# Four edits to the order of one encoder layer's work: a residual load, a fold, a norm and a chain of sums

## The chip, the cores and the metric

The kernel runs on one core of a Trainium2 chip. The time is device microseconds (us) of one execution; for the kernel before it is the median of three runs. The engines are named as the profile names them: PE is TensorE's matmuls, PEld its weight loads, DVE is VectorE, ACT is ScalarE, POOL is GpSimd, and SP is SyncE, which only issues transfers here.

## The reference

One layer of a bidirectional encoder is applied to two groups of tokens with the same weights: "prompt" (1024 tokens) and "sample" (512 tokens), each with 16 meta tokens ahead, which are dropped at the end. Model width 1024, hidden width 4096, fp32.

```python
h = rmsnorm(x, g_mix)
q, k, v, u, gate_na, gate_fn = split(h @ w_in)
y_na = neighbourhood_attention(q, k, v, rel_bias, meta_bias) @ w_branch_na
y_fn = fourier_mix(u) @ w_branch_fn      # real part of a 2-D DFT, positions x channels
mixed = sigmoid(gate_na) * y_na + sigmoid(gate_fn) * y_fn
x = x + mixed @ w_out
a = relu(rmsnorm(x, g_mlp) @ w_up)
y = rmsnorm(x + (a * a) @ w_down, g_final)
```

## The kernel before, in words

Every fp32 product is made of three products of rounded halves (`mm3`, its matmuls at L132): a value x is split into hi = round(x) and lo = x - hi. A weight block of 512 KB is loaded (`weights`, L149, a transfer on SP), cast to hi by ACT (L155), and lo is subtracted by POOL, or by DVE where that is asked for (L157). PE runs almost without a break. There are eight PSUM banks of 512 columns: pairs named ps_mm, ps_s, ps_o and ps_t. Three names (mm, s, o) are handed out in turn to products, and ps_t takes transposes and, in places, products.

`Layer.run` takes the sample first and then the prompt. The stages of the sample are: reading rows with their norm and transposes, attention, `gates` (13 products with columns of w_in, counted from P0), `merge_na` (8 blocks of W_na), the Fourier branch (`fourier_channels`, `fourier_positions`), `merge_fn` (blocks of W_fn and the transposed gate), `project_out` (w_out, the residual, a norm, transposes) and `Up` (32 products f0 to f31 with columns of w_up). The prompt follows with the same stages, and at the end the class `Halves` does the prompt's up projection and the down projection of both groups by a Strassen-like scheme.

The program is written in one order, and a scheduler puts the instructions of each engine into a queue, so what is written late may be queued earlier. Two helpers bind it: `behind(marks)` keeps what is inside it behind the marked instructions, and `pinned()` keeps it behind the last instruction written so far on every engine. Each queue is then worked off strictly in order.

The places that matter here:

- `fold_u` (L248) makes two matrices: a step of loads (the DFT matrix and four blocks of `w_uT`), then eight folds, each of four 128x128 matmuls (L259), three ACT and three DVE evictions and two stores to `wu`. `gates` calls such side steps after its products: a triple (steps, first, end) in `beside` means one step after each product from number `first` up to `end`. `folded` (L869) later loads `wu` back on POOL's queue.
- `merge_na` loads W_na block by block into a tile named relu (L825). `fn_ahead` loads the blocks of `w_fnA` and `w_fnB` (L866), adds and subtracts them and stores the result `wfn` (L860).
- `project_out` adds into four residual tiles `acc` (128x1024, 512 KB each), loaded from the sample's rows at L1091. In the trace these loads stand among W_na's.
- `Up.run` calls `next(reading)` after each pair of products from f2 and f3 on. `reading` is the generator `read` (L277) on the prompt's rows: load a row tile (L288, with a gain load after the first), transpose the tile before (`transpose_in`, L194 on PE, copies at L136 and L137), and `norm` (a square with its sum on ACT at L178, a root at L179, five DVE operations L180 to L184). It has one buffer for the row and one for the normed row. Between these, `combine` loads rows of w_down, subtracts and adds on POOL and stores the sums t2 (L1194).
- `down` (in `Halves`) goes through steps (n, u). A step makes six products, one to a bank. At the last u of an n, each bank is evicted by a DVE add (L1639), and then `load(i + 2)` makes the operands of the step after next: up to four DVE sums of W_down's blocks (L1613, 128x1024), the ACT casts and the POOL or DVE lo parts.

The functions that the change touches, and what calls them:

Of the kernel before, what the change touches and what calls it, by code (L numbers as in the profile page):

```python
# [17 lines left out]
F32 = mybir.dt.float32  # L18
# [8 lines left out]
D = 1024  # L27
# [41 lines left out]
class Layer:  # L69
# [280 lines left out]
    def run(self, order):  # L350
        nc = self.nc
# [3 lines left out]
        hp, close_hT = self.open("hT_0", "left")  # L355
        hT, folded = self.new_hT(hp, order[0][1], NM)
        for i, (name, T) in enumerate(order):
            nxt = order[i + 1] if i + 1 < len(order) else None
            small = T <= 512
# [3 lines left out]
            if i == 0:  # L363
                with pool("first", "right") as p:
                    gain = p.tile([128, D], F32, name="gain")
                    reading = self.read(name, T, hT, lambda: p.tile([128, D], F32, name="xt", bufs=3),
                                        lambda: p.tile([128, D], F32, name="hn", bufs=2), gain)
# [5 lines left out]
                    marks = self.mark((mybir.EngineType.SP,))  # L373
                    w0 = self.qk_weights(0)

                    rest = self.tables(marks)
# [20 lines left out]
            if small:  # L397
                ap, hp_, mp = (right.enter_context(pool(f"{n}_{name}", "right")) for n in ("acc", "hid", "mlp"))
                fn = right_fn.enter_context(pool(f"fn_{name}", "right"))
# [7 lines left out]
            else:  # L407
                fn = None
# [10 lines left out]
            if small:  # L419
                wide = lambda: [fn.tile([128, n], F32R, name=f"wu{n}")[:, :1040].rearrange("p (a b) -> p a b", a=4) for n in (1040, 1072)]  # L420
                flat = lambda pair: [t.rearrange("p a b -> p (a b)") for t in pair]
                beside = [(self.fold_u(mp.tile([128, 512], F32, name="relu", bufs=2)[:, :128],
                                       [t.bitcast(F32) for _ in range(2) for t in flat(self.pair(mp, [128, 2, 512]))],
                                       lambda: flat(self.pair(fn, [128, 4, 128], bufs=4))), 0, 9),
                          (fold, 5, 13)]
            near_end = self.gates(T, hT, mixed, sig, lambda pr: self.weights(
                od[pr], oT[pr], raw=hp_.tile([128, T], F32R, name="hid_hi", bufs=4) if small else "raw"), beside)
            sin = []
# [25 lines left out]
            with self.pinned():  # L454
                for _ in ahead:
                    pass
            if not small:
                close_sin()
            out = ExitStack()
# [13 lines left out]
            if not small:  # L473
# [4 lines left out]
                right_fn.close()  # L478
                Halves(self, name, T).run(right, hp_, mp, h2T, self.wo + rest)
                continue  # L480
            acc = [ap.tile([128, D], F32, name=f"acc{t}") for t in range(T // 128)]
            self.short = mlp = self.Up(self, ap, hp_, mp, name, T, h2T)
            marks = self.mark()
            with self.behind(marks):
                rest = list(wout)
            self.project_out(hp_, mp, self.ins[f"x_{name}"], T, h2T, rest, acc, mlp, marks)
            out.close()
            right_fn.close()
            reading, before_last = iter(()), lambda qs: None
# [591 lines left out]

            yield self.weights(src, place and (place() if callable(place) else self.pair(*place)), lo_engine=self.nc.vector if i == 2 else None)

    def project_out(self, hp, p, x, T, m, wo, acc, mlp, marks):

        nc = self.nc
        wo = self.wo + wo
        nt = T // 128
        gain = self.gain(p.tile([128, D], F32, name="gain", bufs=1), "g_mlp")
        for t in range(nt):  # L1090
            nc.sync.dma_start(acc[t], x[t * 128:(t + 1) * 128, :])  # L1091
        pending = []

        def product(ps, half, t, blocks, more=False):
            ts = slice(t * 128, (t + 1) * 128)
            w = wo[4 * half:4 * half + 4]
            self.mm3(ps, [(m[kt // 2][0][:, kt % 2, ts], m[kt // 2][1][:, kt % 2, ts], w[kt // 2][0][:, kt % 2], w[kt // 2][1][:, kt % 2])
                          for kt in blocks], more=more)
            return ps


        banks = {(0, t): product(self.psum(), 0, t, range(6)) for t in range(2)}
        for half in range(2):
            cs = slice(half * 512, (half + 1) * 512)
            for t in range(nt):
                if (half, t) in banks:
                    ps = product(banks[half, t], half, t, range(6, 8), True)
                else:
                    ps = product(self.psum(), half, t, range(8))
                nc.vector.tensor_tensor(out=acc[t][:, cs], in0=acc[t][:, cs], in1=ps, op=ALU.add)  # L1110
                if half:
                    nc.sync.dma_start(mlp.sums[t], acc[t])
                    if len(pending) == 2:
                        self.transpose_in(*pending.pop(0))
                    hn = hp.tile([128, D], F32, name="hn", bufs=2)
                    self.norm(acc[t], gain, hn, junk=p.tile([128, 512], F32, name="relu", bufs=2).bitcast(BF16))
                    pending.append((hn, m, t * 128))
                    if t == nt - 2:
                        with self.behind(marks):
                            mlp.load(0)  # L1120
        mlp.load(1)
        mlp.load(2)
        for f in range(3):
            next(mlp.ups[f])
            if pending:
                self.transpose_in(*pending.pop(0))

    class Up:
# [68 lines left out]
        def run(self, reading, before_last):  # L1197
            layer = self.layer
            combining = self.combine()
            for g in range(self.NF // 2):  # L1200
                if g == self.NF // 2 - 5:
                    marks = layer.mark()
                if g == self.NF // 2 - 2:
                    for _ in reading:
                        pass
                    for f in range(2 * g, 2 * g + 2):
                        self.load(f)
                    with layer.behind(marks):
                        before_last((0, 1))
                for f in range(2 * g, 2 * g + 2):  # L1210
                    for _ in self.ups[f]:
                        pass
                    if f == self.NF - 2:
                        self.load(f + 1)
                        with layer.pinned():
                            before_last((2, 3))
                with layer.pinned():
                    next(combining, None)
                if g:
                    next(reading, None)  # L1220


class Halves:
# [357 lines left out]
    def down(self, p):  # L1581
# [23 lines left out]
                                    lambda: p.tile([128, 2, TH], F32R, name="long", bufs=2)] + [stream] * 4)  # L1605

        def load(i):
            if i >= len(steps):
                return
            rs, rl, rw, *rest = (x.bitcast(F32) for x in self.raws.pop(i))  # L1610
            n, u = steps[i]
            for x, (_, sign) in zip(rest, self.parts(self.DOWN[n][1], u)[1:]):
                nc.vector.tensor_tensor(out=rw, in0=rw, in1=x, op=ALU.add if sign > 0 else ALU.subtract)  # L1613
            if i < 2:
                x, *others = self.take(5)
                ws = [x[:, k * 2 * SH:(k + 1) * 2 * SH].rearrange("p (a b) -> p a b", a=2) for k in range(2)]
                wl, ww = ([x.rearrange("p (a b) -> p a b", a=2) for x in others[k:k + 2]] for k in (0, 2))
            else:
                ws, wl, ww = (layer.pair(p, [128, 2, w], k, 3) for k, w in (("hs", SH), ("h", TH), ("w", 512)))
            todo = [(rs, ws, nc.vector), (rl, wl, nc.vector), (rw, ww, nc.vector if i == 0 else None)]  # L1620
            done = [layer.split_sb(x, *to, lo_engine=lo) for x, to, lo in (todo if rest else todo[::-1])]
            got[steps[i]] = tuple(done if rest else done[::-1])
# [96 lines left out]
        for i, (n, u) in enumerate(steps):  # L1719
            if u == 0 and n not in self.ON_TOP:  # L1720

                banks = []
                for _ in range(nh):
                    banks.append(layer.psum(("mm", "mm", "s", "s", "t", "t", "o", "o")[used % 8]))
                    used += 1

            with layer.behind(self.stored if i < 6 else []):
                fetch(i + 2)

            if u < nu - 1:  # L1730
                with layer.pinned():
                    load(i + 2)
            if n in (1, 2) and u < nh:
                with layer.pinned():
                    acc[n - 1][u] = self.tile(places[(n - 1) * nh + u])
                    nc.sync.dma_start(acc[n - 1][u], tiles[n - 1][u][0])
            if (n, u) == (3, 0):
                gain = layer.gain(self.tile("gain"), "g_final")
            if n == len(self.DOWN) - 1 and u >= nu - apart:
                continue  # L1740
            for t in range(nh):
                product(banks[t], t, n, [u])
                if u == nu - 1:
                    evict(n, t)
            with layer.pinned():
                if u == nu - 1:
                    load(i + 2)
                elif late:
                    late.pop(0)()
                elif n == 5 and u < nh:  # L1750
                    begin_last(u)
# [90 lines left out]
```

## Time and profile before

| | |
|---|---|
| median of 3 runs | 1930.3 us (1929.49 to 1931.05) |
| the profiled execution's own time | 1930.41 us |
| its span (first to last instruction) | 1928.6 us |
| granted TensorE clock, mean | 0.998 |
| PE busy | 1892.7 us (98%) |
| DVE, ACT, POOL busy | 1117.6, 751.5, 823.2 us |
| moved by DMA | 358.38 MB, 186 GB/s over the span |

1.8 us of the profiled time lie outside the span. In a row of the timeline the first two numbers are the start and the length in us, then come engine, line, operation, output<-inputs, shape and count; in square brackets stands how long the engine had been idle just before and what ended that. "SPq" is SP's queue issuing a transfer. Matmuls overlap in the pipeline, so the start of one row and the end of the row before can cross.

### The profile page before, as it was taken

To read this page: it belongs to the slowest core of one execution; us is meant where nothing else is said; L and a number is where in the kernel's file an instruction comes from. 1 tells how busy PE (TensorE), PEld (TensorE's weight loads), DVE (VectorE), ACT (ScalarE), POOL (GpSimd) and SP (SyncE) were. 2 spreads that over 40 slices of the span, in tenths; PEclk is the share of its full clock that TensorE was granted. 3 is DMA by queue.
4 is the path that set the end of the run, shared out by engine and by line. 5 is a ranking of instruction groups with operands and counts; after the bars stand their busy time and mean duration, and the time that the engine had idled before them with its cause. 6 is when DMAs were issued, how large, how long until landed. Compare 5 with 4: busy or idle time off the path is not lost.

```text
span 1928.6 us, 26107 instructions
## 1 busy us (share of the span) xinstructions
PE 1892.7 (98%) x9435; PEld 1588.4 (82%) x9435; DVE 1117.6 (58%) x1747; ACT 751.5 (39%) x1351; POOL 823.2 (43%) x676
## 2 busy tenths in 40 slices
PE   7999999999999999999999999999999999999998
PEld 5888888888888888888898878888888888888886
DVE  5771554787626566660527375656565326758856
ACT  3674333444215565542223243333333333333334
POOL 1334553555512232342224217988882323323531
PEclk9999999999999999999999999999999999999999
DMA  6757873687765455463452422444446778568733
GB/s 221 195 148 236 228 232 121 213 272 254 237 195 162 125 137 153 136 229 87 129 154 88 164 99 96 179 174 156 174 163 244 274 249 289 199 219 285 273 118 127
DMA packets 312945, 358.38 MB, mean 186 GB/s; under 512 B 51768, under 2 KB 222392, under 8 KB 312264
## 3 DMA queue, kind: packets, MB, share of 16 engines
q1 hardware_dynamic: 295056, 334.93, 52.6%
q0 software_dynamic: 17760, 21.80, 5.0%
q8 instruction: 74, 1.21, 0.3%
q14 instruction: 55, 0.45, 0.1%
HBM read 263.06 MB, written 96.16 MB: 186 GB/s over the span
## 4 chain that ended last, share of the span: by engine, by line
PE 88%; DVE 4%; DMA 3%; ACT 2%; issue 1%; POOL 1%; SPq 0%; DVEq 0%; ACTq 0%; POOLq 0%
PE ps_mm L132 23%; PE ps_o L132 22%; PE ps_s L132 19%; PE ps_t L132 11%; PE ps_mm L531 3%; PE ps_mm L532 3%; PE ps_mm L533 3%; PE ps_o L680 2%; DMA relu<-in_w_na 1%; PE ps_t L660 1%; PE ps_t L194 1%; PE ps_s L647 0%; PE ps_s L648 0%; DMA vf_sample<-vd_sample 0%; DMA gate_prompt<-ot 0%
## 5 line engine op out<-in xcount | busy, mean ns | idle before, releaser
L157 POOL TENSOR_TENSOR w_lo<-w_raw,w_hi 128x1024 fp32r<-128x1024 f32 x69 | 177.1, 2566 | 218.6 <-ACT w_hi L155 160.2
L157 POOL TENSOR_TENSOR w_lo<-raw,w_hi 128x1024 fp32r<-128x1024 f32 (+1 forms) x49 | 100.6, 2056 | 203.3 <-ACT w_hi L155 197.4
L155 ACT CAST w_hi<-w_raw 128x1024 fp32r<-128x1024 f32 x88 | 92.4, 1050 | 175.9 <-PE ps_s L132 48.0
L157 DVE TENSOR_TENSOR h_lo<-long,h_hi 128x1024 fp32r<-128x1024 f32 x54 | 77.2, 1429 | 93.6 <-ACT h_hi L155 93.6
L531 PE MATMUL ps_mm<-hT,w_hi 128*128 128x512 f32 (+2 forms) x296 | 121.5, 410 | 0.0
L532 PE MATMUL ps_mm<-hT,w_hi 128*128 128x512 f32 (+2 forms) x296 | 110.4, 373 | 0.0
L533 PE MATMUL ps_mm<-hT,w_lo 128*128 128x512 f32 (+2 forms) x296 | 110.3, 373 | 0.0
L155 ACT CAST h_hi<-long 128x1024 fp32r<-128x1024 f32 x54 | 56.7, 1050 | 103.2 <-PE ps_s L132 26.7
L157 DVE TENSOR_TENSOR hs_lo<-short,hs_hi 128x512 fp32r<-128x512 f32 x54 | 73.2, 1355 | 13.4 <-ACT hs_hi L155 12.3
L155 ACT CAST w_hi<-raw 128x1024 fp32r<-128x1024 f32 (+1 forms) x49 | 40.9, 840 | 101.6 <-DVE raw L1613 54.4
L654 ACT ACTIVATE sc<-sc,ast 128x288 f32<-128x288 f32 (+4 forms) x96 | 53.9, 561 | 68.3 <-DVE ast L652 68.0
L1397 POOL TENSOR_TENSOR x<-w_hi,x 128x512 fp32r<-128x512 f32 (+1 forms) x42 | 70.9, 1688 | 16.4 <-ACT x L1400 16.4
L680 PEld LDWEIGHTS ps_o<-pt,vb 104*64 104x64 f32 (+6 forms) x576 | 62.4, 163 | 10.1 <-POOL vb L617 2.7
L680 PE MATMUL ps_o<-pt,vb 104*64 104x128 f32 (+6 forms) x576 | 62.3, 243 | 2.1 <-POOL vb L617 1.4
L533 PEld LDWEIGHTS ps_mm<-hT,w_lo 128*128 128x128 f32 x296 | 55.7, 188 | 10.4
L132 PE MATMUL ps_t<-gate,x 128*128 128x512 f32 x264 | 63.7, 390 | 0.0
L617 POOL TENSOR_TENSOR vb<-vr,vb 96x384 fp32r<-96x384 f32 (+4 forms) x48 | 48.5, 1029 | 34.7 <-ACT vb L616 31.1
L132 PE MATMUL ps_mm<-gate,x 128*128 128x512 f32 x256 | 62.6, 389 | 0.0
L774 POOL MEMSET bm<- 64x96 f32 (+2 forms) x64 | 11.1, 174 | 117.7 <-DVE ast L652 103.2
L652 DVE CUSTOM_DVE_ANT_0 sc<-ps_s,bm 128x288 f32<-128x288 f32 (+4 forms) x96 | 46.3, 482 | 23.1 <-issue 10.6
L132 PEld LDWEIGHTS ps_t<-gate,x 128*128 128x128 f32 x264 | 49.4, 188 | 10.9 <-DVE r_lo L1510 0.7
L532 PEld LDWEIGHTS ps_mm<-hT,w_hi 128*128 128x128 f32 x296 | 56.2, 190 | 1.6
(706 smaller groups left out, 5578.6 us busy)
## 6 DMA issues: line engine op xcount, KB each, us to landing
long<-hidden_prompt SPq DMA_DIRECT2D x54, 512.0 KB
w_raw<-in_w_in SPq DMA_DIRECT2D x52, 512.0 KB
raw<-in_w_down SPq DMA_DIRECT2D x39, 512.0 KB
w_raw<-in_w_up SPq DMA_DIRECT2D x34, 512.0 KB
hidden_prompt<-h SPq DMA_DIRECT2D x32, 512.0 KB
short<-hidden_sample SPq DMA_DIRECT2D x54, 256.0 KB
w_lo<-in_w_down SPq DMA_DIRECT2D x18, 512.0 KB
w_raw<-in_w_out SPq DMA_DIRECT2D x16, 512.0 KB
```

Of the source, the lines that this page charges most:

```text
L132: self.nc.tensor.matmul(out, a, b, start=(i == 0 and not more), stop=(i == len(terms) - 1), skip_group_check=more)
L155: nc.scalar.copy(out=hi, in_=raw)
L157: (lo_engine or nc.gpsimd).tensor_tensor(out=lo, in0=raw, in1=hi.bitcast(F32), op=ALU.subtract)
L194: nc.tensor.transpose(tp[:, i * 128:i * 128 + n], hn[:n, kt * 128:(kt + 1) * 128], self.ident[:n, :n])
L531: nc.tensor.matmul(ps, a[0], b[0], start=(kt == 0), stop=False)
L532: nc.tensor.matmul(ps, a[0], b[1], start=False, stop=False)
L533: nc.tensor.matmul(ps, a[1], b[0], start=False, stop=(kt == 7))
L617: nc.gpsimd.tensor_tensor(out=lo, in0=vs, in1=hi.bitcast(F32), op=ALU.subtract)
L652: nc.vector.tensor_tensor_reduce(out=sc[:, :W], in0=ps[:, :W], in1=bm[:, :W], scale=1.0, scalar=3e38, op0=ALU.add, op1=ALU.min, accum_out= ...
L654: nc.scalar.activation(out=sc[:, :W], in_=sc[:, :W], func=AF.Exp, bias=st[:, 0:1], scale=-1.0, accum_out=st[:, 1:2])
L680: nc.tensor.matmul(po[:m, j * 128:(j + 1) * 128], v, x, start=(i == 0), stop=(i == len(ops) - 1))
L1397: self.nc.gpsimd.tensor_tensor(out=to, in0=x, in1=y, op=op)
```

## The change

Four edits, in four places:

1. `fold_u`'s loads stay behind product P0 of the sample's gates; its eight folds stand behind P2 to P9 instead of P1 to P8.
2. The sample's four residual row tiles are loaded in `run`, right after the last step of `fn_ahead` and pinned there, instead of in `project_out`, from where the scheduler had drawn them forward.
3. In `Up.run` the call of `next(reading)` after f3 (g = 1) is bound behind the last instructions written so far on SP, ACT, POOL and DVE. That call loads the prompt's first row tile and norms it.
4. In `down`, the sums of `load(i + 2)` at the last u of an n are made one after each eviction, pinned there, instead of all after the sixth eviction. The casts and lo parts stay behind the last sum.

```diff
-                beside = [(self.fold_u(mp.tile([128, 512], F32, name="relu", bufs=2)[:, :128],
+                beside = [self.fold_u(mp.tile([128, 512], F32, name="relu", bufs=2)[:, :128],
                                        [t.bitcast(F32) for _ in range(2) for t in flat(self.pair(mp, [128, 2, 512]))],
-                                       lambda: flat(self.pair(fn, [128, 4, 128], bufs=4))), 0, 9),
-                          (fold, 5, 13)]
+                                       lambda: flat(self.pair(fn, [128, 4, 128], bufs=4)))]
+                beside = [(*beside, 0, 1), (*beside, 2, 10), (fold, 5, 13)]
...
             with self.pinned():
                 for _ in ahead:
                     pass
+                if small:
+                    acc = [ap.tile([128, D], F32, name=f"acc{t}") for t in range(T // 128)]
+                    for t in range(T // 128):
+                        nc.sync.dma_start(acc[t], self.ins[f"x_{name}"][t * 128:(t + 1) * 128, :])
...
-            acc = [ap.tile([128, D], F32, name=f"acc{t}") for t in range(T // 128)]
             self.short = mlp = self.Up(self, ap, hp_, mp, name, T, h2T)
...
-            self.project_out(hp_, mp, self.ins[f"x_{name}"], T, h2T, rest, acc, mlp, marks)
+            self.project_out(hp_, mp, T, h2T, rest, acc, mlp, marks)
...
-    def project_out(self, hp, p, x, T, m, wo, acc, mlp, marks):
+    def project_out(self, hp, p, T, m, wo, acc, mlp, marks):
...
-        for t in range(nt):
-            nc.sync.dma_start(acc[t], x[t * 128:(t + 1) * 128, :])
...
                 if g:
-                    next(reading, None)
+                    with layer.behind(layer.mark() if g == 1 else []):
+                        next(reading, None)
...
         def load(i):
+            for _ in load_parts(i):
+                pass
+
+        def load_parts(i):
...
                 nc.vector.tensor_tensor(out=rw, in0=rw, in1=x, op=ALU.add if sign > 0 else ALU.subtract)
+                yield
...
+            loading, sums = iter(()), 0
+            if u == nu - 1 and i + 2 < len(steps):
+                loading = load_parts(i + 2)
+                sums = len(self.parts(self.DOWN[n + 1][1], 1)) - 1
             for t in range(nh):
                 product(banks[t], t, n, [u])
                 if u == nu - 1:
                     evict(n, t)
+                    if t < sums:
+                        with layer.pinned():
+                            next(loading, None)
             with layer.pinned():
                 if u == nu - 1:
-                    load(i + 2)
+                    for _ in loading:
+                        pass
```

Three places show what this does to the queues; the line numbers are of the kernel whose order it is.

**PE in the sample's `Up`, around f5 and f6.** gate holds the normed hidden input, r the prompt's normed row tile 0. Before:

```order
L132 MATMUL ps_mm<-gate,w_hi 128x512 x16
L132 MATMUL ps_mm<-gate,w_lo 128x512 x8
L194 MATMUL ps_t<-ident,r_3972 128x128 x8
L132 MATMUL ps_s<-gate,w_hi 128x512 x16
L132 MATMUL ps_s<-gate,w_lo 128x512 x8
```

and in the changed kernel:

```order
L132 MATMUL ps_mm<-gate,w_lo 128x512 x8
L132 MATMUL ps_s<-gate,w_hi 128x512 x16
L132 MATMUL ps_s<-gate,w_lo 128x512 x3
L194 MATMUL ps_t<-ident,r_3972 128x128 x8
L132 MATMUL ps_s<-gate,w_lo 128x512 x5
L132 MATMUL ps_o<-gate,w_hi 128x512 x16
```

The eight transposes of the prompt's first row tile stood ahead of f6 and now stand after 19 of its 24 matmuls. Those of the second and third tile stand inside f8 and f10 in the same way (after 19 and 7 matmuls); from the fourth tile on they stand between products, as before.

**SP in the sample's `Up`.** Before, the first row's load (L288) stood among the sums' stores at the end of `project_out`:

```order
L1112 DMA sum_sample_3360<-acc_3348 128x1024
L1112 DMA sum_sample_3361<-acc_3349 128x1024
L288 DMA r_3969<-in_x_prompt 128x1024
L170 DMA r_3830<-in_g_mix 128x1024
L1112 DMA sum_sample_3362<-acc_3350 128x1024
L149 DMA w_raw<-in_w_up 128x8x128 x2
L288 DMA r_4061<-in_x_prompt 128x1024
L1168 DMA hidden_sample_3351<-hid_hi 128x2x256
```

and in the changed kernel:

```order
L1169 DMA hidden_sample_3355<-hid_lo 128x2x256
L1177 DMA hidden_sample_3355<-hn 128x4x256
L1195 DMA t_0_3893<-acc_3895 128x512
L288 DMA r_3969<-in_x_prompt 128x1024
L170 DMA r_3830<-in_g_mix 128x1024
L1169 DMA hidden_sample_3356<-hid_hi 128x2x256
L149 DMA w_raw<-in_w_up 128x8x128 x2
```

The first row's load now stands behind the stores of the second pair (f2, f3) and behind the first store of t2.

**SP at the end of the Fourier branch.** acc is a residual tile, gain at the first row a buffer that holds half of W_fn's rows. In the changed kernel:

```order
L869 DMA gain<-in_w_fnB 128x4x128
L460 DMA acc_3151<-in_x_sample 128x1024
L460 DMA acc_3152<-in_x_sample 128x1024
L863 DMA wfn_3145<-raw 128x512
L863 DMA wfn_3149<-raw 128x512
L460 DMA acc_3153<-in_x_sample 128x1024
L460 DMA acc_3154<-in_x_sample 128x1024
L149 DMA w_raw<-in_w_out 128x2x512 x2
L170 DMA gain<-in_g_mlp 128x1024
L149 DMA w_raw<-in_w_out 128x2x512 x6
```

The four residual loads stood two and two between W_na's last blocks (issued at 229.58 and 233.32 us in the trace before; the W_fn row that opens this piece was issued at 269.87), and one w_out load stood directly behind that W_fn row. Now all four stand ahead of every w_out load.

## The prediction

> **What bounds the kernel now.** I read the page first, its busy times and its chain.
>
> ```profile
> span 1928.6 us, 26107 instructions
> PE 1892.7 (98%) x9435; PEld 1588.4 (82%) x9435; DVE 1117.6 (58%) x1747; ACT 751.5 (39%) x1351; POOL 823.2 (43%) x676
> PE 88%; DVE 4%; DMA 3%; ACT 2%; issue 1%; POOL 1%; SPq 0%; DVEq 0%; ACTq 0%; POOLq 0%
> ```
>
> PE is busy for 98% of the span and makes 88% of the chain. None of the four edits takes a matmul away, so all they can win is idle time of PE, of which there is little. The view of waits, PE's rows alone, says how much of it lies where the edits are:
>
> ```profile
> PE ps_mm L259 <- DMA w_hi<-in_w_uT: 1.5, 1, 1.5
> PE ps_t L132 <- POOL w_lo L157: 1.2, 1, 1.2
> PE ps_s L132 <- ACT hid_hi L155: 1.1, 1, 1.1
> PE ps_t L194 <- DVE gate L137: 0.9, 1, 0.9
> ```
>
> Each stands for one wait (us in total, times, longest). PE's timeline places them, always the row before and the row that waited:
>
> ```profile
> 157.97 1.07 PE L132 MATMUL ps_s<-hT,w_hi 128*128 128x512 f32 x4
> 160.56 0.46 PE L259 MATMUL ps_mm<-relu,w_hi 128*128 128x128 f32 x2 [1.52 <-DMA w_hi<-in_w_uT]
> ...
> 245.03 1.07 PE L132 MATMUL ps_mm<-oT_hi,hid_lo 128*128 128x512 f32 x4
> 247.20 0.50 PE L132 MATMUL ps_s<-oT_hi,hid_hi 128*128 128x512 f32 x1 [1.10 <-ACT hid_hi L155]
> ...
> 348.49 0.72 PE L132 MATMUL ps_mm<-gate,w_hi 128*128 128x256 f32 x4
> 350.11 0.63 PE L194 MATMUL ps_t<-ident,hn 128*128 128x128 f32 x4 [0.89 <-DVE gate L137]
> ...
> 1731.99 0.39 PE L132 MATMUL ps_t<-w_hi,h_hi 128*128 128x512 f32 x1
> 1733.55 0.50 PE L132 MATMUL ps_t<-w_lo,h_hi 128*128 128x512 f32 x1 [1.17 <-POOL w_lo L157]
> ```
>
> The idle times add to 1.52 + 1.10 + 0.89 + 1.17 = 4.68 us. Counted from start to start they are a little larger, since matmuls overlap: later rows give a start every 0.233 us (16 matmuls of f6 from 378.02 to 381.75, quoted below), so that the first wait, 160.56 - 157.97 - 4 x 0.233, cost 1.66, the second 1.24, the last 1.33. With about 1.0 for the third that is 5.2. It is the most that the change can win.
>
> **The change part by part.**
>
> *The fold.* The first fold waits for `w_uT`. One gates product later is 24 matmuls x 0.233 = 5.6 us, more than the 1.52 that are missing: -1.66. The other side: the stores of `wu` come up to 5.6 us later. Between the last fold and the Fourier products that need `wu` stand three products (16.8 us) and eight W_na blocks of 12 matmuls (22.4 us), which hide a store and a load. The loads of `wu` stand in POOL's queue, however, and the lo parts behind them wait with them; I bound that by 0 and 2 us and take 0, since POOL is busy for 43% only.
>
> *The residual rows.* The second wait ends with the cast of W_na's last block, and the queue and the chain show why that block is late:
>
> ```profile
> 229.58 1.03 SPq L1091 DMA_DIRECT2D acc<-in_x_sample  x2
> 233.32 1.08 SPq L1091 DMA_DIRECT2D acc<-in_x_sample  x2
> 236.29 10.14 DMA relu<-in_w_na
> ```
>
> Its load was issued behind four 512 KB rows of the residual and took 10.14 us to land. With the rows gone from there 1.24 us are won. In their new place they stand ahead of all of w_out:
>
> ```profile
> 275.81 1.05 ACT L155 CAST w_hi<-w_raw 128x1024 fp32r<-128x1024 f32 x1 [2.17 <-DMA w_raw<-in_w_out]
> 286.29 0.38 SPq L149 DMA_DIRECT2D w_raw<-in_w_out  x1
> 290.03 1.06 ACT L155 CAST wo_hi<-w_raw 128x1024 fp32r<-128x1024 f32 x1 [0.35 <-DMA w_raw<-in_w_out]
> 294.39 0.39 PE L132 MATMUL ps_o<-w_hi,gate 128*128 128x512 f32 x1
> ```
>
> The first w_out block is cast at 275.81 and first used at 294.39. Two megabytes at the 294 GB/s of a full stretch (window row below) are 7.1 us, so the first block is still 8 us early with its lo part. Later blocks wait for buffers more than for data; the fourth is cast at 290.03. I take 0.2 for the one of them that might come late, with 0 and 2 as bounds.
>
> *The first norm.* In the third wait PE's transposes of the sample want a copy from DVE, and DVE is busy with the prompt's first norm, one row of which is
>
> ```profile
> 347.15 1.27 DVE L184 SCALAR_TENSOR_TENSOR r<-r,st,r 128x1024 f32<-128x1024 f32 x1
> ```
>
> With the norm out of that place about 1.0 is won. But the row's load goes with it, and PE's transposes of that row now stand inside f6. Here lies the main cost. The rows for it:
>
> ```profile
> 374.73 0.33 SPq L1194 DMA_DIRECT2D t<-acc  x1
> 377.23 1.03 PE L194 MATMUL ps_t<-ident,r 128*128 128x128 f32 x8
> 378.02 3.89 PE L132 MATMUL ps_s<-gate,w_hi 128*128 128x512 f32 x16
> 381.75 1.98 PE L132 MATMUL ps_s<-gate,w_lo 128*128 128x512 f32 x8
> ...
> 388.44 0.41 SPq L288 DMA_DIRECT2D r<-in_x_prompt  x1
> 393.61 1.06 ACT L178 ACTIVATE r<-r 128x1024 f32<-128x1024 f32 x1 [2.85 <-DMA r<-in_x_prompt]
> 396.30 1.28 DVE L184 SCALAR_TENSOR_TENSOR r<-r,st,r 128x1024 f32<-128x1024 f32 x1
> ...
> 383.83 3.50 DVE L184 SCALAR_TENSOR_TENSOR r<-r,st,r 128x1024 f32<-128x1024 f32 x1
> 383.86 2.40 POOL L157 TENSOR_TENSOR w_lo<-w_raw,w_hi 128x1024 fp32r<-128x1024 f32 x1 [3.60 <-PE ps_s L132]
> ```
>
> When PE is there: f6 can start at 377.23, where the transposes no longer stand, and 19 matmuls x 0.233 later it is 381.7. When the row is there: its load is issued behind the store of t2 (374.73 + 0.33 = 375.1). From issue to the square it took 5.2 us in the third row's case (388.44 to 393.61); a w_out load of the same 512 KB took 3.7 (286.29 to 290.03). From the square's start to the end of L184 it was 4.0 us (393.61 to 397.58). So the row is ready at 382.8 to 384.3, if DVE lets the norm's steps through at once. In the changed order six operations of f4 and f5 stand between them, of which I count 1.2 as not fitting into the norm's own waits: 384.0 to 385.5, and PE stalls for 2.3 to 3.8. L184 took 3.50 instead of 1.28 where POOL's w_lo ran beside it; that w_lo waited for f6's end, and the transposes now stand ahead of that end, so this does not add here. The bounds are 1.1 (no DVE delay, fast load) and 7.3 (slow load, slow L184); I take 3.5. ACT and DVE have the eviction of f5 behind that norm, which only the turn of banks needs.
>
> The second and third row have one buffer each for load and norm, so a row's load waits for the norm before it. One round is 5.2 + 4.0 = 9.2 us and about a microsecond in SP's queue, say 10.2; PE's slots are 48 matmuls (5 of f6, 24 of f7, 19 of f8) and the transposes' 0.8, 12.0 us, and then 5 + 24 + 7 = 36, 9.2 us. The second fits, the third is late by about 1.0 less the 1.8 that the second has spare, or more where L184 runs beside POOL. Bounds 0 and 4; I take 1.5.
>
> *The sums.* The last wait is behind this sequence, of DVE, ACT and POOL:
>
> ```profile
> 1717.23 0.69 DVE L1639 TENSOR_TENSOR u<-u,ps_t 128x512 f32<-128x512 f32 x1 [8.58 <-PE ps_t L132]
> ...
> 1728.65 1.22 DVE L1613 TENSOR_TENSOR raw<-raw,w_hi 128x1024 f32<-128x1024 f32 x1
> 1729.98 1.06 ACT L155 CAST w_hi<-raw 128x1024 fp32r<-128x1024 f32 x1 [13.89 <-DVE raw L1613]
> 1731.11 2.38 POOL L157 TENSOR_TENSOR w_lo<-raw,w_hi 128x1024 fp32r<-128x1024 f32 x1 [19.77 <-ACT w_hi L155]
> ```
>
> The third sum starts after all six evictions. If three sums follow the first three evictions, the last of them can be through near 1717.23 + 3 x (0.69 + 1.22) = 1723, some 6 us sooner, and the wait of 1.33 is gone. The evictions come up to 1.7 us later; a bank is next needed a round of six products later, so this costs nothing. -1.33.
>
> The sum: -1.66 - 1.24 - 1.0 - 1.33 = -5.2; +3.5 + 1.5 + 0.2 = +5.2. The profiled execution (1930.41: span 1928.6 and 1.8 around it) would stay at 1930.4, and since it lies 0.1 above the median, that is **1930.3** for the median.
>
> **The rivals.** A change of 0.2%, 3.9 us, is about the least that a measurement of this kernel tells from none, so 1926.4 and 1934.2 are the limits of "the same".
>
> *A: the prompt's rows are in time.* Then nearly all of the gain stays: 1930.3 - 5.2 + 0.2 to + 1.2 = 1925.3 to 1926.3, say 1925.7, faster. For it: the load could land sooner than the 3.7 us, since few transfers run there, and the stall of the first row alone could be at its lower bound. Against it: the order behind the store is fixed, and even the lower bound leaves 1.1.
>
> *B: the late rows pull each other.* If L184 runs beside POOL for each of the first three rows, the first stall is 7.3 and the next ones make 4.0; the point from which this decides is a norm that takes over 8 us from square to L184's end. Such idle time also costs clock. After gaps of 1.02 and 2.13 us the trace shows it:
>
> ```profile
> 1148.23 0.63 PE L1274 MATMUL ps_s<-ident,h 128*128 128x128 f32 x4 [1.02 <-DVE gate L137]
> 1150.98 1.09 PE L1274 MATMUL ps_t<-ident,x 128*128 128x128 f32 x4 [2.13 <-DVE gate L137]
> ...
> 1145.00:1152.00 7.00, 3.85 (x27) 3.30 (x27) 5.89 (x14) 4.31 (x13) 1.26 (x1) 0.92 0.92 294
> 1152.00:1156.00 4.00, 4.00 (x17) 3.21 (x15) 3.02 (x7) 1.61 (x5) 0.00 (x0) 0.72 0.01 4
> ```
>
> (The last three numbers of a window row are the granted clock, the DMA share and GB/s.) At 0.92 for 7 us and 0.72 for 4 us, 0.56 + 1.12 = 1.7 us of PE's work are lost. Sum: -5.2 + 7.3 + 4.0 = +6.1, with one such loss of clock 1930.3 + 7.8 = 1938.1 at the most; half of the excess over my main terms is the likelier size, 1934.5 to 1936, slower. Against it: POOL's w_lo waits for PE's own progress, which keeps it away from the first norm. The Trainium skill (TensorE: Matmul & The Clock Gate, section "What's actually happening") says that the array's clock is halved after an idle window of about 3.4 us whose phase is free; by that rule a stall of 3.5 us falls into one whole window seldom, and would then cost another 1.7 us for one window at half speed. The window rows above agree with a halved clock for some microseconds, after idle time in two pieces.
>
> *C: w_out or the lo parts behind `wu` come late.* The main case with the two other bounds: 1930.3 + 2 to + 3 = 1932.8, the same. For it: the block at 290.03 still waited 0.35 for its data. Against it: 8 us of cover for the first block.
>
> *D: the change doesn't do what it says.* W_na's last block may stay late, because W_fn's loads and the folds' stores share the same engines; 1.24 less is won: 1931.5, the same.
>
> **How the numbers follow.** Main case 0.48 (its own range 1927.5 to 1933.5), A 0.24, B 0.16, C 0.07, D 0.05. Faster: A's larger part and the low end of the main case, where the two stalls stay near 1.1 and 0: 0.27. Slower: B and a little of the main case's high end, 0.18. The same: 0.55. The range from A's low end to near B's likelier size, 1925.3 to 1935.2, leaves out less than 2 in 10.
>
> **What would show it.** Right: no wait for `w_uT`, for W_na's cast near 247, for the norm near 350 and for w_lo near 1733; a new wait of PE at L194 for DVE's r (L184) inside f6, 2 to 4 us long, and a smaller one inside f10. The row's load should stand on SP right behind the store of t2. Wrong: no wait inside f6 (then A), waits in f6, f8 and f10 with a granted clock under 0.9 behind them (B), waits for w_out near 295 (C), a wait that remains at W_na's eighth block (D). The whole is wrong if PE's idle time in the four places does not go, or if a stage that no edit touches moves.

## The result and the profile after

The changed kernel takes 1941.87 us (median of 6 runs, 1939.25 to 1944.56) against 1930.4 us before (6 runs, 1929.49 to 1931.05): a ratio of 1.0059, 95% interval 1.0049 to 1.0069. It is slower by about 11.5 us, outside the range, and by more than rival B allowed. The profiled execution took 1941.83 us, 11.42 more than the one before.

The page of the changed kernel:

```profile
span 1940.1 us, 26128 instructions
PE 1897.3 (98%) x9435; PEld 1591.7 (82%) x9435; DVE 1113.3 (57%) x1747; ACT 752.9 (39%) x1351; POOL 819.3 (42%) x676
```

PE's busy time grew from 1892.7 to 1897.3 us with the same 9435 matmuls: 4.6 us. So the matmuls themselves ran slower somewhere. The other 6.8 us of the 11.42 are idle time of PE. In the view of waits the four rows quoted in the prediction are all gone, and of those over 0.5 us one has come, four times and 11.5 us in all:

```profile
PE ps_t L194 <- DVE r L184: 11.5, 4, 4.0
```

11.5 us came and 4.68 us went: 6.8. PE's timeline shows where the four are; the last row stands for the matmuls behind the fourth:

```profile
378.68 1.06 PE L194 MATMUL ps_t<-ident,r 128*128 128x128 f32 x8 [2.52 <-DVE r L184]
...
393.79 1.06 PE L194 MATMUL ps_t<-ident,r 128*128 128x128 f32 x8 [1.50 <-DVE r L184]
...
406.55 1.23 PE L194 MATMUL ps_t<-ident,r 128*128 128x128 f32 x8 [3.48 <-DVE r L184]
...
422.56 1.94 PE L194 MATMUL ps_t<-ident,r 128*128 128x128 f32 x8 [4.02 <-DVE r L184]
424.15 5.60 PE L132 MATMUL ps_s<-gate,w_hi 128*128 128x512 f32 x16
```

They are the first four of the prompt's rows, and all inside or right behind f6, f8, f10 and f11. The sixteen matmuls at 424.15 took 5.60 us where the same sixteen took 3.79 to 3.89 before. The windows over this stretch show why (granted clock third from the end of a row):

```profile
380.00:400.00 20.00, 18.50 (x79) 14.89 (x79) 14.10 (x17) 6.51 (x11) 10.23 (x5) 0.91 0.67 219
400.00:420.00 20.00, 15.06 (x63) 11.85 (x61) 12.90 (x17) 8.57 (x14) 8.92 (x5) 0.91 0.67 206
420.00:440.00 20.00, 17.44 (x74) 14.66 (x75) 12.50 (x16) 8.23 (x14) 5.88 (x3) 0.83 0.56 173
```

Before, the clock was 1.00 in these stretches. Everything else is as it was: no wait of PE for w_out, none for `wu`, none in the down projection that was not there before. The loss lies between 375 and 430 us.

The way of the rows through the queues, in the changed kernel. First their loads on SP, with the store of t2 ahead of the first:

```profile
368.91 0.33 SPq L1195 DMA_DIRECT2D t<-acc  x1
369.41 0.34 SPq L288 DMA_DIRECT2D r<-in_x_prompt  x1
...
379.22 0.41 SPq L288 DMA_DIRECT2D r<-in_x_prompt  x1
...
393.71 0.53 SPq L288 DMA_DIRECT2D r<-in_x_prompt  x1
...
407.49 0.42 SPq L288 DMA_DIRECT2D r<-in_x_prompt  x1
```

then their squares on ACT, the second with the cast that stands ahead of it:

```profile
373.59 1.06 ACT L178 ACTIVATE r<-r 128x1024 f32<-128x1024 f32 x1 [2.41 <-DMA r<-in_x_prompt]
...
386.24 1.05 ACT L155 CAST w_hi<-w_raw 128x1024 fp32r<-128x1024 f32 x1 [4.05 <-PE ps_o L132]
387.20 1.05 ACT L178 ACTIVATE r<-r 128x1024 f32<-128x1024 f32 x1
...
400.35 1.06 ACT L178 ACTIVATE r<-r 128x1024 f32<-128x1024 f32 x1 [3.69 <-DMA r<-in_x_prompt]
...
413.63 1.05 ACT L178 ACTIVATE r<-r 128x1024 f32<-128x1024 f32 x1
```

and the ends of their norms on DVE, with two operations on the fourth row's way:

```profile
377.26 1.28 DVE L184 SCALAR_TENSOR_TENSOR r<-r,st,r 128x1024 f32<-128x1024 f32 x1
...
392.36 1.28 DVE L184 SCALAR_TENSOR_TENSOR r<-r,st,r 128x1024 f32<-128x1024 f32 x1
...
405.12 1.28 DVE L184 SCALAR_TENSOR_TENSOR r<-r,st,r 128x1024 f32<-128x1024 f32 x1
...
413.76 2.43 DVE L1165 TENSOR_TENSOR hid_hi<-hid_hi 128x512 f32<-128x512 f32 x1 [4.31 <-ACT hid_hi L1164]
...
418.83 2.26 DVE L183 SCALAR_TENSOR_TENSOR st<-st 128x1 f32<-128x1 f32 x1
421.12 1.28 DVE L184 SCALAR_TENSOR_TENSOR r<-r,st,r 128x1024 f32<-128x1024 f32 x1
```

Each load is issued 0.1 to 1.1 us after the norm of the row ahead has ended (378.54, 393.64, 406.40): there is one row buffer. From one norm's end to the next the rounds take 15.1, 12.8 and 16.0 us. The prediction had 10.2. The rows above split each round into the time to the load's issue, from there to the square, and from the square to the norm's end: 0.7 + 8.0 + 6.4, 0.1 + 6.6 + 6.1 and 1.1 + 6.1 + 8.8 us, where the prediction had 1.0 + 5.2 + 4.0. The middle part is not the load alone: in the second and fourth row the square stood on ACT behind work that waited for PE (the cast at 386.24), while in the third ACT waited 3.69 us for the load itself.

### The profile page after: what moved, and what is told of

Read it like the earlier page. It is cut to its first block, busy times and chain, and to the rows that moved or that the text cites. A ratio compares the mean times of both kernels' runs of the same rounds, so it can differ in the third digit from the quotient of the medians.

```text
span 1940.1 us, 26128 instructions
## 1 busy us (share of the span) xinstructions
PE 1897.3 (98%) x9435; PEld 1591.7 (82%) x9435; DVE 1113.3 (57%) x1747; ACT 752.9 (39%) x1351; POOL 819.3 (42%) x676
## 4 chain that ended last, share of the span: by engine, by line
PE 90%; DVE 4%; DMA 3%; issue 1%; ACT 1%; POOL 0%; SPq 0%; DVEq 0%; POOLq 0%; ACTq 0%
PE ps_mm L132 23%; PE ps_o L132 23%; PE ps_s L132 19%; PE ps_t L132 11%; PE ps_mm L534 3%; PE ps_mm L535 3%; PE ps_mm L536 3%; PE ps_o L683 2%; PE ps_t L663 1%; PE ps_t L194 1%; DMA r<-in_x_prompt 1%; PE ps_s L651 1%; PE ps_s L650 1%; DMA vf_sample<-vd_sample 0%; DMA bm<-g_un 0%
## 5 line engine op out<-in xcount | busy, mean ns | idle before, releaser
L157 DVE TENSOR_TENSOR hs_lo<-short,hs_hi 128x512 fp32r<-128x512 f32 x54 | 63.8, 1181 | 16.9 <-ACT hs_hi L155 16.9
```

The costliest lines, as they stand in the source:

```text
L157: (lo_engine or nc.gpsimd).tensor_tensor(out=lo, in0=raw, in1=hi.bitcast(F32), op=ALU.subtract)
```

## Experiments

Each kernel was timed beside the kernel before on the same chip. On these chips the kernel before takes 1928.7 to 1929.1 us, so ratios are compared, not times.

### Which of the four edits costs

The changed kernel without the third edit, and the kernel before with the third edit alone:

```diff
-                    with layer.behind(layer.mark() if g == 1 else []):
-                        next(reading, None)
+                    next(reading, None)
```

> The changed kernel with its third edit taken back (the prompt's first norm isn't bound; the fold, the residual rows and the sums stay as changed). Theory 1, the whole loss comes from the bound: no wait of PE for the prompt's rows (L194 for r), the waits for w_uT, W_na's cast and w_lo stay away, the one for the norm near 350 comes back with 0.9 us, granted clock 0.998, time 1930.4 - 1.66 - 1.24 - 1.33 = 1926.2 us. Rival, the residual rows' new place makes the loads of the next stage late and the rows with them: PE waits over 2 us for rows or w_out remain, 1932 us or more.

```diff
-                    next(reading, None)
+                    with layer.behind(layer.mark() if g == 1 else []):
+                        next(reading, None)
```

> The kernel before with the third edit alone. Theory 1: the four waits for the prompt's rows (11.5 us) and the lost clock (4.6 us) appear here too, the one near 350 goes (1.0): 1930.4 + 11.5 + 4.6 - 1.0 = 1945.5 us. Rival, the residual rows share in it: under 1936 us.

Without the third edit: 1925.14 us, ratio 0.9982 (0.9973 to 0.9991). With it alone: 1944.93 us, ratio 1.0085 (1.0068 to 1.0101). In the views of waits the first has only the old wait near 350 of those in question, and the second has the four new ones:

```profile
PE ps_t L194 <- DVE gate L137: 0.9, 1, 0.9
```

```profile
PE ps_t L194 <- DVE r L184: 12.1, 4, 4.0
```

The whole loss comes from the bound call; the rival, that the residual rows in their new place share in it, falls. The other three edits together win 3.5 us (1.7 to 5.2 by the interval) where 4.2 were expected.

### Each of the other three alone

> The kernel before with the first edit alone. If the prediction's term is right: no wait for w_uT (L259), nothing new, 1.0 to 1.7 us less. Rival, the later stores of wu hold up POOL's queue: a new wait of PE for a lo part or for wu, no gain.

> The kernel before with the second edit alone. If the term is right: no wait for W_na's last cast, no wait for w_out, 0.3 to 1.2 us less. Rival, the 2 MB only move the lateness to the W_fn and w_out loads: a new wait of 0.5 us or more between 260 and 300 us, no gain or a loss.

> The kernel before with the fourth edit alone. If the term is right: no wait of PE for the lo part near 1733, nothing new in the down projection, 1.3 us less. Rival, the evictions that now stand behind sums hold banks longer: new waits of PE in the down projection, no gain.

The edits are the pieces of the change's diff for `fold_u`, for `acc` and `project_out`, and for `down`. Measured ratios: fold 0.9997 (0.9988 to 1.0006), rows 0.9995 (0.9986 to 1.0004), sums 0.9992 (0.9983 to 1.0001). No single one of them is clear of no change, which fits gains of about a microsecond each. Their traces say more than their times. With the fold alone no wait for `w_uT` is left; with the sums alone none for w_lo near 1733; with the rows alone none for W_na's cast, while with the fold alone these two rows stand for it:

```profile
PE ps_s L132 <- ACT hid_hi L155: 0.6, 1, 0.6
PE ps_mm L132 <- ACT hid_hi L155: 0.4, 1, 0.4
```

None of the three traces has a new wait of over 0.2 us at the places the rivals named. On these chips the waits taken away were smaller than in the trace before: with the rows alone the one for `w_uT` reads

```profile
PE ps_mm L259 <- DMA w_hi<-in_w_uT: 0.9, 1, 0.9
```

instead of 1.5, and in the kernel with the third edit alone, on another chip, this one and the one for W_na's cast read 1.0 and 0.3. So the terms -1.66 and -1.24 look like upper ends rather than middles.

### Where the loss starts: the load or the norm

The third edit holds back both the row's load (SP) and its norm (ACT, DVE). Three kernels split it; the changed kernel ran beside two of them.

```diff
-                    with layer.behind(layer.mark() if g == 1 else []):
+                    with layer.behind(layer.mark((mybir.EngineType.SP,)) if g == 1 else []):
```

> The changed kernel, but the first call on the prompt's rows is bound on SP alone: the row's load stays behind the store of t2, the norm's operations on ACT and DVE are free. Theory 1, the late load starts the loss: the four waits stay as they are (11.5 us, within 0.5), the time is that of the changed kernel within 2 us. Rival, the norm's place in the queues of ACT and DVE starts it: the waits fall under 6 us.

```diff
-                    with layer.behind(layer.mark() if g == 1 else []):
+                    with layer.behind(layer.mark((mybir.EngineType.Activation, mybir.EngineType.DVE)) if g == 1 else []):
```

> The mirror of it: the first call is bound on ACT and DVE, the row's load is free and goes out early. Theory 1: no waits for the prompt's rows and none for the norm near 350, 3.5 to 4.5 us below the kernel before. Rival: waits of 2 us or more at the first row, 2 us or more above the kernel before.

```diff
-                    with layer.behind(layer.mark() if g == 1 else []):
+                    with layer.behind(layer.mark((mybir.EngineType.DVE,)) if g == 1 else []):
```

> The changed kernel, but the first norm is bound behind the last instruction of DVE alone, so that the row's load and the square on ACT may come early and only the five DVE operations stay out of the transposes. Theory 1 with the late load as its start: no waits for the prompt's rows and none of the four old ones, 1930.4 - 5.2 = 1925.2 us, up to 1926.2 if the square on ACT still costs at the transposes. Rival, rounds of 13 to 16 us a row are too long for PE's slots of 12 wherever they start: waits of 1 to 4 us at rows 1 to 3, 1931 us or more.

> The changed kernel itself beside the next three, so that they are compared on one chip. Both theories: 11 to 14 us above the kernel before, with four waits for the prompt's rows of 11 to 12 us in all and a granted clock of 0.993 to 0.996.

The load alone bound: 1940.6 us, ratio 1.0065 (1.0043 to 1.0086), and 12.2 us in the four waits. The changed kernel on that chip: 1939.46, 1.0053 (1.0034 to 1.0073), with 9.8 us in the four waits and a granted clock of 0.998 in its profiled execution, both a little off what was expected. The norm alone bound: 1925.37, 0.9980 (0.9971 to 0.9990); DVE's part alone bound: 1925.15, 0.9981 (0.9972 to 0.9990); in both no wait for a prompt row is left, nor the one near 350. Both are faster than the kernel before and than the changed one. So holding the norm out of the transposes does what it should, and the loss starts with the load that goes behind the store of t2 along with it. Against the kernel without the third edit (0.9982) the two win nothing that can be measured, though their traces lack its wait of 0.9 us. In both kernels the scheduler also put the transposes between products again, 48 matmuls apart, so that the short slots are gone along with the late load; the next section takes the slots apart.

In the kernel with the norm bound, all eight norms pass through the same one row buffer without a wait of PE. The view of line L184 there gives their number, shortest, median and longest time, and first and last start:

```profile
L184 DVE SCALAR_TENSOR_TENSOR r<-r,st,r x8: 1283/1284/1286, 369.9 to 450.0; 128x1024 f32<-128x1024 f32 x8
```

That is 80.1 us for seven rounds, 11.4 each on average, under PE's slot of 11.8 there (transposes at 372.09 and 383.86). Single rounds took 8.6 to 14.2 us, and each norm ended only 0.5 to 3.8 us ahead of its transposes. So the single buffer keeps up, but with little to spare for a row that starts late.

### Why the lateness repeats

The prediction let only the first row be late in earnest. What makes the second, third and fourth late too? Two buffers in turn, in place of the one:

```diff
-                reading = self.read(*nxt, hT, lambda: tile_("r0").bitcast(F32), lambda: tile_("r2").bitcast(F32), tile_("r3").bitcast(F32))
+                reading = self.read(*nxt, hT, lambda turn=[0]: (turn.__setitem__(0, 1 - turn[0]), tile_(f"r{1 - turn[0]}").bitcast(F32))[1], lambda: tile_("r2").bitcast(F32), tile_("r3").bitcast(F32))
```

> The changed kernel, but the prompt's rows are loaded into two buffers in turn (r0 and r1) instead of one, so that a load no longer waits for the norm ahead of it. Theory 1a, the single row buffer makes rows 1 to 3 late: only the first row's wait of 2.5 us and up to 3 at the second are left, with one stretch of half clock: 1941.9 - 9.0 + 1.5 - 3.1 = 1931 us. Theory 1b, the norm's own path through ACT's and DVE's queues, which stand behind PE's products, sets the rounds: three or four waits remain, 1937 us or more.

1933.51 us, ratio 1.0025 (1.0014 to 1.0035), against 1.0059 of the changed kernel. Two waits are left, 6.3 us in all; rows three and four are in time. The second row was waited for although its load had not been late: with a buffer of its own the scheduler had drawn it forward to 333.33 us. Its square on ACT stood behind the copies of the first row's transposes (382.89), and on DVE two operations ran beside POOL's lo parts (L1165 2.42 us, L184 3.34). So a late row delays the next one through these queues too. The scheduler had also moved the transposes in this kernel (the second row's stand 29 matmuls behind the first row's, the later ones 48), so the slots were another reading of the same result. The next kernel keeps one buffer and gives every row an even slot of 48 matmuls, right behind f6, f8, f10 and so on. The edit moves the whole call, so from the second row on the loads and norms are written later as well:

```diff
             if last:
-                self.transpose_in(*last)
+                with self.behind(self.after):
+                    self.transpose_in(*last)
...
                     for _ in self.ups[f]:
                         pass
+                    if g > 2 and f == 2 * g:
+                        layer.after = layer.mark((mybir.EngineType.PE,))
+                        next(reading, None)
...
-                if g:
-                    with layer.behind(layer.mark() if g == 1 else []):
+                if g == 1:
+                    with layer.behind(layer.mark()):
                         next(reading, None)
```

> The changed kernel with its late load and its one row buffer, but the transposes of the prompt's rows bound to PE's queue right after f6, f8, f10 and so on: 48 matmuls apart each, where the changed kernel has 48, 36 and 41; the first stands 5 matmuls later than there. Theory 2a, the short slots pull rows 2 and 3 late: the first wait is 2.5 - 1.1 = 1.4 us, the others under 1 us in all, 1 us below to 2 us above the kernel before. Theory 2b, a round of one row through one buffer takes 12.8 to 16 us whatever the slots: waits of 1 to 4 us at rows 1 to 3 remain, 7 us or more above the kernel before.

1957.05 us, ratio 1.0146 (1.0129 to 1.0163): far worse, and theory 2a falls. What the later place of the loads and norms adds was not tried alone. Six rows are waited for; in PE's timeline the fourth and the sixth read

```profile
427.96 1.94 PE L195 MATMUL ps_t<-ident,r 128*128 128x128 f32 x8 [8.58 <-DVE r L185]
...
459.49 1.94 PE L195 MATMUL ps_t<-ident,r 128*128 128x128 f32 x8 [5.02 <-DVE r L185]
```

The load that the fourth row waited for shows another way in which rows hang together. Its buffer was free at 407.26 (end of L185), but on SP it stood behind stores that waited for DVE:

```profile
410.09 0.37 SPq L1171 DMA_DIRECT2D hidden_sample<-hid_lo  x1
...
413.20 0.41 SPq L1171 DMA_DIRECT2D hidden_sample<-hid_hi  x1
413.66 0.47 SPq L289 DMA_DIRECT2D r<-in_x_prompt  x1
```

Last, the same even slots and the same late first load with two buffers:

> The evenly slotted kernel (transposes of the prompt's rows right after f6, f8, f10 and so on, late first load) with two row buffers in turn instead of one. Theory 2b, a round through one buffer (load behind norm, norm behind load) is what repeats the wait: only the first row's wait of 1.6 us is left, with at most one stretch of half clock: 1929.1 - 3.7 + 1.6 + 0 to 1.7, 1927 to 1929 us. Rival, the stores ahead of the loads on SP and the evictions ahead of the norm on DVE set the rounds whatever the buffers: waits of over 3 us at two rows or more, 1940 us or more.

1926.08 us, ratio 0.9984 (0.9975 to 0.9993). One wait is left, the first row's:

```profile
PE ps_t L195 <- DVE r L185: 1.4, 1, 1.4
```

Between these two kernels lie 31 us, and their code differs in one row buffer. On SP that buffer does two things:

```profile
333.94 0.42 SPq L289 DMA_DIRECT2D r<-in_x_prompt  x1
...
372.12 0.34 SPq L289 DMA_DIRECT2D r<-in_x_prompt  x1
...
384.56 0.41 SPq L289 DMA_DIRECT2D r<-in_x_prompt  x1
```

The load at 372.12 is the first row's, behind the store of t2 (its square follows at 376.34). The one at 333.94 is the second row's, drawn forward because its buffer is free, and each later load may go out behind the norm two rows ahead instead of the one just ahead. So it is the single buffer, with its ring "load behind the norm ahead of it, norm behind the load", that hands a late first row's lateness on; how much the early second row does and how much the freedom of the later loads was not separated. The ring alone did no harm: with the norm bound and the load early it kept up with PE. With a late first row there was too little to spare, and rounds of 12.8 to 16.0 us followed until one of 7.7 us at the fifth row (L184 at 421.12 and 428.81 in the changed kernel). Rows queued on ACT behind a cast that waited for PE's product (386.24 above), on DVE beside POOL (L1165 2.43 instead of the 0.69 us that the same operation took at 375.26), and, in the evenly slotted kernel, on SP behind stores (413.66 above). What each of these queues alone would cost was not tried.

## Why the prediction was wrong

*What bounds the kernel, and the four gains.* Right: PE's idle time was all there was to win, all four waits went, and nothing was lost where they had been. The kernels with the norm or DVE bound, which have all four gains and no late row, win 3.7 us (1.9 to 5.6). The 5.2 taken lies within that; the traces of the single edits, in which two of the waits were shorter, suggest less.

*The fold, the residual rows, the sums.* Right in each cover that was named: no wait for `wu`, for w_out or for a bank showed up. The 0.2 for w_out was not needed. Rivals A, C and D did not happen.

*The first row.* Right in mechanism and size: 3.5 was taken, 2.52 was measured. Its load went out right behind the store of t2, took 4.2 us to the square (3.7 to 5.2 expected), and the norm 5.0 us from there (4.0 and 1.2 for the operations between).

*The second and third row.* This step failed. "One round is 5.2 + 4.0 = 9.2 us and about a microsecond in SP's queue, say 10.2" put together the shortest way through idle queues; the rounds took 15.1, 12.8 and 16.0. It took the 4.0 from a row for which ACT had been waiting; in the changed order the square of the second row stood behind the cast at 386.24, and the norms shared DVE with evictions and POOL and took 6.4, 6.1 and 8.8 us from the square. The term was 1.5 with 4 as its upper bound; by the prediction's own numbers the third row was 1.0 late less 1.8 spare, so the 1.5 was a margin and not worked out. Rows two and three took 1.50 + 3.48 = 5.0, and the fourth, which the prediction didn't count at all because its transposes stand between products as before, took 4.02 more. (A small misreading lies beside it: 0.233 us a matmul comes from a row right behind transposes. Plain rows give 0.227, 3.63 us for the sixteen from 383.56 to 387.19 in the trace before, so a slot is up to 0.3 us shorter.) A row's place between products says nothing when the row ahead of it hands its lateness on.

*POOL beside DVE.* The argument that w_lo "waits for f6's end" and so keeps away from the norm held for the first row (L184 took 1.28). It was no argument for the next ones: in the second row's norm L1165 took 2.20 us (388.86), in the third's L182 took 2.02 (402.86), and in the fourth's L1165 at 413.76 and L183 at 418.83 took 2.43 and 2.26, each beside a lo part on POOL. The Trainium skill (SBUF — State Buffer, section "Who interferes with whom") says that a DVE operation with two SBUF inputs contends with POOL's reads; 2.43 against 0.69 us for L1165 agrees with it.

*The clock.* This term was put at nothing in the main case and at one loss of 1.7 us in rival B. Measured are 4.6 us of longer matmuls, over three stretches at 0.91, 0.91 and 0.83. The sentence on the Trainium skill's rule, by which "a stall of 3.5 us falls into one whole window seldom", was the wrong way to use it: the clock fell behind a stall of 2.52 us already. Read as a whole window of about 3.4 us without work (TensorE: Matmul & The Clock Gate, section "What's actually happening"), the rule would rule that out; the measurement decides, and a stall shorter than the window can cost clock. The last section shows when.

*Rival B* named the sign, the lateness that passes from row to row and the lost clock, with a chance of 0.16. The cause that it gave did not happen: L184 took 1.28 us in each of the four rows, other operations ran beside POOL, and the norms took 5.0 to 8.8 us, only the fourth over its limit of 8. Its highest sum, 1938.1, had stalls of 7.3 + 4.0 = 11.3 us, close to the 11.5 measured, though it put most of them on the first row, where 1.3 of its 7.3 us have no row behind them; it fell short by 3.8, of which 2.9 are clock (4.6 against 1.7) and 0.5 the gains (4.7 against 5.2). But I took half of its excess as the likelier size. The measured terms add to 1930.4 - 4.7 + 11.5 + 4.6 = 1941.8. They are not independent: at half clock PE needed 13.6 us from the first transposes to the second wait, where the even slot takes 11.8, and came to that wait later.

## What to carry to other kernels

A bound that keeps work out of one place also holds back everything issued with it, its load first of all: bind only the engine that gets in the way, and let the load go early. Where a stream runs through a single buffer, add up one round with the queues as they will then be, not the shortest way through empty ones, and ask how much a late row could make up; here a second buffer did what even slots did not. And price idle time of PE with clock on top, by how much of it can fall into one stretch of 3.4 us (next section).

## What the runs showed that was not expected

The same waits do not cost the same. Most kernels with late rows spread more widely than those without: the kernel with only the third edit took 1938.35 to 1948.51 us, the changed kernel 1935.45 to 1942.97 on another chip, while the one without the third edit took 1922.72 to 1926.73. The evenly slotted kernel with one buffer is an exception, with 1955.59 to 1957.75. Two profiled executions on the same chip, of the changed kernel and of the one with the load alone bound, took 1935.45 and 1947.04 us, with four such waits each, of 9.8 and 12.2 us. Their pages read, in this order,

```profile
PE 1892.6 (98%) x9435; PEld 1588.3 (82%) x9435; DVE 1109.5 (57%) x1747; ACT 752.8 (39%) x1351; POOL 820.2 (42%) x676
```

```profile
PE 1899.9 (98%) x9435; PEld 1593.9 (82%) x9435; DVE 1111.1 (57%) x1747; ACT 753.2 (39%) x1351; POOL 819.6 (42%) x676
```

PE is busy for 7.3 us longer in the second, for the same matmuls, at a granted clock of 0.994 against 0.998. In kernels without such waits it is busy for 1890.7 to 1892.7 us, so the first lost at most 2 us to the clock and the second 7 to 9.

What decides this can be read from the traces. In the changed kernel's first profile the clock is at half from 380.00 to 383.41, from 407.31 to 410.72 and from 420.96 to 427.79, that is for 3.41, 3.41 and twice 3.41 us, and the later stretches begin 8 and 12 times 3.41 us after the first. So the clock changes on a grid of 3.41 us. The two executions above have such stretches too, and their grids lie elsewhere: they begin at 406.02 us in the first and at 381.40 in the second. The Trainium skill (TensorE: Matmul & The Clock Gate, section "What's actually happening") says that the clock's window runs freely and does not start with the kernel; the traces agree.

These are windows of the grid in the changed kernel's first profile; PE's busy time stands second in a row and the granted clock third from the end:

```profile
376.59:380.00 3.41, 1.32 (x10) 1.31 (x11) 1.98 (x5) 1.70 (x3) 0.00 (x0) 1.00 1.07 334
380.00:383.41 3.41, 3.41 (x9) 2.65 (x9) 2.44 (x3) 1.02 (x2) 1.72 (x1) 0.50 1.04 357
...
390.24:393.65 3.41, 2.04 (x10) 1.34 (x8) 3.40 (x8) 1.05 (x1) 0.27 (x1) 1.00 0.46 104
393.65:397.07 3.42, 3.29 (x19) 2.88 (x20) 1.67 (x3) 1.68 (x3) 0.91 (x1) 1.00 1.10 385
...
403.89:407.31 3.42, 0.76 (x7) 0.79 (x8) 3.32 (x5) 0.10 (x1) 0.98 (x1) 1.00 0.26 72
407.31:410.72 3.41, 3.41 (x11) 2.73 (x10) 2.11 (x5) 1.08 (x2) 0.00 (x0) 0.50 1.05 316
...
417.55:420.96 3.41, 0.98 (x5) 0.48 (x3) 3.34 (x5) 0.90 (x2) 3.41 (x2) 1.00 0.66 188
420.96:424.37 3.41, 1.81 (x9) 1.84 (x10) 2.09 (x4) 0.59 (x1) 0.11 (x1) 0.50 0.24 56
```

A window with 2.1 us or more of idle time (busy for 1.32, 0.76 or 0.98) is followed by one at half clock, and the window with 1.4 us (busy for 2.04) is not. So it matters where a stall falls. In the profile of 1935.45 us the first stall is longer, 2.85 us, but lies in two windows with 1.4 and 1.5 us and costs no clock; only its third, of 3.43 us, has 3.0 us in one window, and there is one stretch at half clock. In the evenly slotted kernel a stall of 3.70 us, split into 1.7 and 2.0, costs none either. The profile of 1947.04 us has three stretches at half clock between 380 and 435 us, two of them of twice 3.41 us. These figures hold for the stretch in which the rows are late; at about 1161 us in the changed kernel, where PE does short transposes, 1.7 us of waits in a window were enough.
